# A state space layer between dense layers on one core: its stages in another order, and the norm factor applied when two of its quarters leave PSUM

## The chip, the cores and the metric

The kernel runs on one core of a Trainium2 chip. A core has a matrix engine (TensorE: PE in the profile, its weight loads PEld), a vector engine (VectorE: DVE), an engine for activations and copies (ScalarE: ACT), GpSimd (POOL) and a queue engine (SyncE: SP). Matrix products are written to PSUM, which VectorE and ScalarE read; everything else lies in SBUF or in HBM, and DMA queues of SP, ACT and POOL move data between these. The metric is the device time of one execution in microseconds (us), as the median of several runs; lower is better.

## The reference, cut to what matters

A sequence of 256 tokens of width 1024 goes through a stack of mixers and feed-forward layers. The third mixer is the state space layer:

```
def s5_layer(xn, w_in, ...):
    u = (xn @ w_in)                                   # 1024 channels = 64 groups of 16
    bu = einsum(bbar, u per group)                    # 64 complex states per group
    x[t] = a * x[t-1] + bu[t]                         # per group and state, over the tokens
    y = einsum(c_re, x_re) - einsum(c_im, x_im) + d_skip * u
    hg = gelu(y) @ w_glu
    a, g = split(hg, 2)
    return a * sigmoid(g)
```

`xn` is the RMS-normed input: `x` times a factor per token, times a gain per channel. The factor per token can be applied behind `@ w_in`, and the kernel does that.

## The kernel before, in words

**Dense products.** All matrix products with large weights run in three float32r passes. `mm3` (lines 514 to 518) multiplies a 128 x 128 block by a high and a low part of the activations, and the low part of the block by the high part of the activations, 256 tokens each. A *unit* is 8 blocks (512 KB). Units are loaded in the order of the list `s.plan` from SP's queue into five staging buffers `st`. A unit that isn't *raw* is then split into `wh` by ScalarE (line 374) and `wl` by VectorE (line 375), which frees its staging buffer; a raw unit is read by TensorE from the staging buffer and holds it until then.

**Who orders the work.** The program is written as one sequence of instructions. A list scheduler puts each engine's instructions in order: of those that are ready in its own plan of time it takes the one that stands first in the program, so a later one can move ahead while an earlier one waits. Each engine then runs its instructions strictly in that order. `keep_in_program_order` (not used in the layer before) forbids that an instruction is put ahead of the one that stands just before it on its engine. Matmuls into one PSUM bank stay in program order.

**The state space layer** (`s5`, lines 1205 to 1344) treats the 1024 channels as four quarters q of 256 channels (16 groups), and as two halves h of two quarters. `S5SEQ` (line 49) is the order of its stages, and `plan_s5` (line 1164) lists the weight units in the same order:

- **G q** (`g_stage`, line 1235): u = yh, yl times `w_in` for one quarter, 16 blocks. ScalarE copies PSUM to `uT` in another column order (line 1249), its queue stores that in HBM (`dU`, line 1250), and POOL's queue loads it back as `U8[q]` (line 1252), which turns the layout: tokens in steps of eight go to the partitions.
- **R** (`r_stage`, line 1227): the norm factor per token, `rrow` (256 values on every partition), and `r8`, the same in the layout of `U8`.
- **B q** (`b_stage`, line 1255): `U8[q]` times `r8` (VectorE, line 1258); 32 small products with raw units of `dB` into `Z` (line 1266); then a chain of eleven VectorE operations (lines 1273 to 1287): a turn by cosine and sine, two scans, a turn back, and the states written to `S[q]`. Its tiles `a`, `b`, `d` exist once, so the chains of two quarters can't overlap.
- **T h** (`y_mm(h, True)`, line 1299): what tokens within a group of eight do to each other, from `U8` of both quarters of the half, into `Y[h]`.
- **C h** (`y_mm(h, False)`, line 1303): the part from the states, `S` of both quarters, with raw units of `dC`, added to `Y[h]`.
- **F h** (`fin`, line 1306): gelu of `Y[h]` (ScalarE, line 1309), then for each half b of the tokens 4 products with the identity into the one buffer `pz` (line 1314), and from there the high and low parts `oh`, `ol` (`hilo`, lines 542 and 543). The second b needs `pz` back.
- **O** (`glu`, line 1323): the product with `w_glu`, 128 blocks (384 matmuls). The blocks stand in `glu_order` (line 138): 24 blocks that need only the first half of `oh`, for three output tiles; 24 that need the second half, for the same tiles; then the other five tiles. The three tiles hold the three PSUM buffers `mm` until their second 24 blocks are done. `ev_g` (line 1332) makes the result of a tile and adds it to `x`.

The next layer's feed-forward product follows; its matmuls need `x`.

Of the kernel before, what the change touches and what calls it, by code (L numbers as in the profile page):

```python
# [14 lines left out]
OP = mybir.AluOpType  # L15
# [30 lines left out]
PSTEP = (24, 36)  # L46
FSIDE = ((0.2, 0.8, 15), (1.6, 0.2, 16))
SIDE = (0, 1, 1.6, 0.6, 1.4, 0.2, 0.8, 1.0)
S5SEQ = [(x[0], int(x[1])) for x in "G0 G1 G2 R0 B0 G3 B1 T0 B2 B3 T1 C0 F0 C1 F1 O0 O1 O2".split()]
MAGIC = float(1.5 * 2 ** 23)  # L50
PI = float(np.pi)
INV2PI = float(1.0 / (2 * np.pi))
C1 = 6.28125
# [230 lines left out]
class Build:  # L284
# [879 lines left out]
    def plan_s5(s):  # L1164
        nc = s.nc
        s.dE = s.dp.tile([8, 64, 2, 64], F32, tag="dE", name="dE")
        s.dU = [s.dp.tile([8, 128, 64], F32, tag="dU%d" % q, name="dU") for q in range(4)]
        s.dB = s.dp.tile([8, 128, 8, 128], F32, tag="dB", name="dB")
        s.dC = s.dp.tile([8, 128, 8, 128], F32, tag="dC", name="dC")
        s.dK = s.dp.tile([64, 32, 2, 128], F32, tag="dK", name="dK")  # L1170
        def op(src, n):
            def f(st):
                s.pre_step(1e9)
                nc.sync.dma_start(st.rearrange("p (a n) -> p a n", a=n), src)
            return f

        for kind, q in S5SEQ:
            if kind == "G":
                for k in (2 * q, 2 * q + 1):
                    ap = s.I["s5in"]  # L1180
                    s.plan.append((ap[k], ap.shape[2], False))
            elif kind == "B":
                for k in (2 * q, 2 * q + 1):
                    s.plan.append((op(s.dB[k], 8), UW, True))
            elif kind == "C":
                v = s.dC[q * 4:q * 4 + 4].rearrange("k p g n -> p k (g n)")
                for m in range(4):
                    s.plan.append((op(v[:, :, m * 256:m * 256 + 256], 4), UW, True))
            elif kind == "O":
                for k in ((0, 3), (3, 6), (6, 16))[q:q + 1]:  # L1190
                    for u in range(*k):
                        s.plan.append((s.I["s5glu"][u], UW, False))

# [11 lines left out]
    def s5(s, nxt):  # L1205
        nc = s.nc
        mm = nc.tensor.matmul
        tt, stt = nc.vector.tensor_tensor, nc.vector.scalar_tensor_tensor
        with s.tc.tile_pool(name="s5", bufs=1) as fp, s.tc.tile_pool(name="s5w", bufs=1) as w5:
            f = lambda shape, tag, dt=F32: fp.tile(shape, dt, tag=tag, name=tag)  # L1210
            uT = [f([128, 1024], "uy%d" % h) for h in range(2)]
            uT = [uT[q // 2][:, (q % 2) * 512:(q % 2) * 512 + 512].rearrange("p (j k c) -> p j k c", j=8, k=2)
                  for q in range(4)]
# [21 lines left out]
            def g_stage(q):  # L1235
                P = s.ps().rearrange("p (k t) -> p k t", k=2)
                late = []
                for k in range(2):
                    for c in range(KC):
                        w = s.blk()  # L1240
                        if q or c < 6:
                            s.mm3(P[:, k], w, s.yh[:, c], s.yl[:, c], k == 0 and c == 0, c == KC - 1)
                        else:
                            late.append((k, c, w))
                    if q * 2 + k in NSTEP:
                        next(pre, None)
                for k, c, w in late:
                    s.mm3(P[:, k], w, s.yh[:, c], s.yl[:, c], False, c == KC - 1)
                nc.scalar.copy(uT[q].rearrange("p j k c -> p k j c"), P.rearrange("p k (c j) -> p k j c", j=8))
                nc.scalar.dma_start(s.dU[q].rearrange("j p n -> p j n"), uT[q].rearrange("p j k c -> p j (k c)"))  # L1250
                u = s.dU[q]
                nc.gpsimd.dma_start(U8[q].rearrange("p g k c -> p (g k c)"),
                                    bass.AP(tensor=u.tensor, offset=u.offset, ap=[[512, 16], [8192, 8], [1, 512]]))

            def b_stage(q):

                u = U8[q].rearrange("p g k c -> p (g k) c")
                tt(u, u, r8.unsqueeze(1).to_broadcast([128, 16, 32]), OP.mult)
                Z = (s.ps() if q % 2 else s.pz.tile([128, 512], F32, tag="pz", name="pz"))
                Z = Z.rearrange("p (r n) -> p r n", r=2)  # L1260
                for pr in range(8):
                    w = [s.blk(), s.blk()]
                    gg = pr * 2
                    for ri in range(2):
                        for half in range(2):
                            mm(Z[64 * half:64 * half + 64, ri, pr * 32:pr * 32 + 32],
                               w[half][:, ri * 64:ri * 64 + 64], U8[q][:, gg % 8 + half, gg // 8],
                               start=pr == 0 and ri == 0, stop=True, skip_group_check=True)
                sl = slice(q * 8, q * 8 + 8)
                Zv = Z.rearrange("p r (a c) -> p r a c", a=8)  # L1270
                cs, sn = [z[:, sl].unsqueeze(1).to_broadcast([128, 2, 8, 32]) for z in (s.s5cos, s.s5sin)]
                a, b, d = [w5.tile([128, 2, 8, 32], F32, tag=n, name=n) for n in "abd"]
                tt(b, Zv, cs, OP.mult)
                tt(d, Zv, sn, OP.mult)
                tt(a[:, 0], b[:, 0], d[:, 1], OP.add)
                tt(a[:, 1], b[:, 1], d[:, 0], OP.subtract)
                fl = lambda z: z.rearrange("p a c -> p (a c)")
                for r in range(2):
                    nc.vector.tensor_tensor_scan(fl(a[:, r]), fl(dec[:, sl]), fl(a[:, r]), 0.0, OP.mult, OP.add)
                Sv = S[q][:, :, 1:33].rearrange("p (a g) c -> p a g c", g=2)  # L1280
                R = [slice(0, 64), slice(64, 128)]
                tt(b, a, cs, OP.mult)
                tt(d, a, sn, OP.mult)
                for half, r in enumerate(R):
                    tt(Sv[0:64, :, half], b[r, 0], d[r, 1], OP.subtract)
                for half, r in enumerate(R):
                    tt(Sv[64:128, :, half], d[r, 0], b[r, 1], OP.add)

            def y_mm(h, direct):

                if direct:
                    Y[h] = s.zt().rearrange("p b (g n) -> p (b g) n", g=4)
                for g in range(8):
                    if not direct and g % 2 == 0:
                        w = s.unit()
                    for k in range(4):
                        q, e = 2 * h + k // 2, k % 2
                        if direct:
                            mm(Y[h][32 * k:32 * k + 32, g], U8[q][:, g, e], s.dT[h][:, k * 8 + g],
                               start=g % 4 == 0, stop=False, skip_group_check=True)  # L1300
                        else:
                            o = (k * 2 + g % 2) * 128
                            mm(Y[h][32 * k:32 * k + 32, g], S[q][:, e * 8 + g, 0:32], w[:, o:o + 128],
                               start=False, stop=True, skip_group_check=True)

            def fin(h):

                yg = f([128, 1024], "uy%d" % h).rearrange("p (j n) -> p j n", j=8)
                nc.scalar.activation(yg.rearrange("p j (g h) -> p g j h", g=8),
                                     Y[h].rearrange("p g (j h) -> p g j h", j=8), AF.Gelu_apprx_tanh)  # L1310
                for b in range(2):
                    P = s.pz.tile([128, 512], F32, tag="pz", name="pz")
                    for j in range(4):
                        mm(P[:, j * 128:j * 128 + 128], yg[:, b * 4 + j], s.c["ident"], start=j == 0, stop=True,
                           skip_group_check=True)
                    k, t = slice(4 * h, 4 * h + 4), slice(128 * b, 128 * b + 128)
                    v = lambda z: z[:, k, t].rearrange("p k (j c) -> p j k c", j=4)
                    s.hilo(v(oh), v(ol), P.rearrange("p (j k c) -> p j k c", j=4, k=4))
# [3 lines left out]

            def glu(k):

                for j, m, c in order[24 * k:24 * k + 24 if k < 2 else None]:
                    if j not in PG:
                        PG[j] = s.ps().rearrange("p (m t) -> p m t", m=2)
                    s.mm3(PG[j][:, m], s.blk(), oh[:, c], ol[:, c], m == 0 and c == 0, c == KC - 1)
                    if m and c == KC - 1:
                        ev_g(j, PG[j])  # L1330
# [614 lines left out]
```

## Time and profile before

| what | us |
|---|---|
| median of 3 runs (1617.16 to 1620.99) | 1618.54 |
| the profiled execution, device time | 1625.3 |
| the profiled execution, first to last instruction (the span all times below are counted from) | 1623.2 |
| first G stage to the last GLU tile, in that span | about 597 to 703 |
| TensorE busy, share of the span | 97% |

All rows come from the profiled execution. In a timeline a row is: start, duration, engine, line, operation, what it writes and reads, count; in brackets stands how long the engine was idle before it, and what released it. A record of a small matmul (lines 1266, 1299, 1303, 1314) is one of two passes, so 32 products give 64 records. The clock column of a table of windows (PEclk) is the granted clock of TensorE: 1.00 is 2.4 GHz, 0.50 is 1.2 GHz.

### The profile page before, as it was taken

Reading aid. Unit: us, or ns where it says so; the run is one execution under the profiler, and the core shown is the slowest. Engines: PE = TensorE matmul, PEld = TensorE weight load, DVE = VectorE, ACT = ScalarE, POOL = GpSimd, SP = SyncE. Lnnn points to the kernel's source line nnn. Section 1 sums busy time; section 2 is a strip of 40 time slices with the busy share of each in tenths; the row PEclk is TensorE's granted clock in tenths of the full one; section 3 lists DMA queues with packets and bytes.
Section 4 is the critical chain, followed back from the end, with each engine's and each line's share of the span. In section 5 each row is a group of like instructions: output and inputs, shape, how many; then the busy total and the mean of one; then the engine's idle time right before and its main releaser. Section 6 shows DMA issues by size and latency. Waiting matters only on the chain.

```text
span 1623.2 us, 33910 instructions
## 1 busy us (share of the span) xinstructions
PE 1573.0 (97%) x13644; PEld 1510.7 (93%) x13644; DVE 1303.4 (80%) x2380; ACT 948.1 (58%) x1481; POOL 64.1 (4%) x110
## 2 busy tenths in 40 slices
PE   7999999989999997999999999999999999999998
PEld 6999999979898996999999999999997899999998
DVE  8989998979889887788888567988886667766667
ACT  6777565645446661665556676656665546554444
POOL 0320100011110000000000000000000000000000
PEclk9999999999999998999999999999999999999999
DMA  7655666597986657746555434565553434656662
GB/s 262 202 181 176 230 212 223 201 279 228 244 245 227 219 186 221 258 165 215 195 195 184 167 118 157 190 200 195 173 171 125 151 119 132 202 193 195 194 196 79
DMA packets 95229, 312.54 MB, mean 193 GB/s; under 512 B 14928, under 2 KB 20560, under 8 KB 95072
## 3 DMA queue, kind: packets, MB, share of 16 engines
q1 hardware_dynamic: 82560, 282.21, 52.5%
q0 software_dynamic: 8352, 27.12, 5.9%
q8 instruction: 107, 1.75, 0.4%
q10 hardware_dynamic: 4160, 1.05, 0.3%
q14 instruction: 50, 0.41, 0.1%
HBM read 297.49 MB, written 12.85 MB: 191 GB/s over the span
## 4 chain that ended last, share of the span: by engine, by line
PE 72%; issue 10%; DVE 9%; DMA 6%; ACT 3%; POOL 0%; DVEq 0%; ACTq 0%; POOLq 0%; SPq 0%
PE mm L516 16%; PE mm L517 15%; PE mm L518 15%; PE z L516 5%; PE z L517 5%; PE z L518 5%; DVE wl L375 3%; DMA st<-ffn_dram 2%; DMA A<-s5bT_dram 2%; PE mm L530 1%; PE mm L531 1%; PE mm L529 1%; ACT wh L374 1%; PE z L818 1%; PE z L805 1%
## 5 line engine op out<-in xcount | busy, mean ns | idle before, releaser
L375 DVE TENSOR_TENSOR wl<-st,wh 128x1024 fp32r<-128x1024 f32 x508 | 617.1, 1218 | 156.9 <-ACT wh L374 156.1
L374 ACT CAST wh<-st 128x1024 fp32r<-128x1024 f32 x508 | 528.6, 1046 | 338.8 <-PE mm L517 206.8
L516 PE MATMUL mm<-yh,wh 128*128 128x256 f32 x2512 | 702.8, 280 | 1.6 <-ACT yh L568 0.9
L518 PE MATMUL mm<-yh,wl 128*128 128x256 f32 x2512 | 698.0, 278 | 4.4 <-DVE wl L375 4.4
L517 PE MATMUL mm<-yl,wh 128*128 128x256 f32 x2512 | 697.4, 278 | 1.0 <-DVE yl L569 0.6
L516 PEld LDWEIGHTS mm<-yh,wh 128*128 128x128 f32 x2512 | 472.6, 188 | 9.2 <-issue 6.0
L518 PEld LDWEIGHTS mm<-yh,wl 128*128 128x128 f32 x2512 | 473.2, 188 | 5.6 <-DVE wl L375 5.4
L517 PEld LDWEIGHTS mm<-yl,wh 128*128 128x128 f32 x2512 | 473.3, 188 | 2.5 <-DVE yl L569 1.0
L516 PE MATMUL z<-hh,wh 128*128 128x256 f32 x880 | 243.7, 277 | 0.0
L517 PE MATMUL z<-hl,wh 128*128 128x256 f32 x880 | 243.3, 276 | 0.4 <-DVE hl L543 0.4
L518 PE MATMUL z<-hh,wl 128*128 128x256 f32 x880 | 242.4, 276 | 1.3 <-DVE wl L375 1.3
L518 PEld LDWEIGHTS z<-hh,wl 128*128 128x128 f32 x880 | 164.9, 188 | 1.5 <-DVE wl L375 1.5
L516 PEld LDWEIGHTS z<-hh,wh 128*128 128x128 f32 x880 | 165.1, 188 | 1.1 <-issue 0.4
L517 PEld LDWEIGHTS z<-hl,wh 128*128 128x128 f32 x880 | 165.2, 188 | 0.7 <-DVE hl L543 0.6
L727 DVE SCALAR_TENSOR_TENSOR cv<-pr,conv,cv 128x255 f32<-128x255 f32 (+1 forms) x352 | 146.8, 477 | 1.3 <-ACT cv L725 0.9
L542 ACT CAST hh<-hm 128x256 fp32r<-128x256 f32 x110 | 44.5, 405 | 124.0 <-DVE hm L732 99.0
L725 ACT ACTIVATE cv<-pr,conv 128x256 f32<-128x256 f32 x176 | 95.8, 593 | 14.7 <-DVE pr L722 14.7
L516 PE MATMUL mm<-oh,wh 128*128 128x256 f32 x320 | 89.9, 282 | 0.0
L517 PE MATMUL mm<-ol,wh 128*128 128x256 f32 x320 | 88.3, 277 | 0.0
L518 PE MATMUL mm<-oh,wl 128*128 128x256 f32 x320 | 88.2, 277 | 0.0
L722 DVE TENSOR_TENSOR pr<-mm,rrow 128x512 f32<-128x512 f32 x88 | 60.1, 687 | 13.2 <-PE mm L518 12.9
L543 DVE TENSOR_TENSOR hl<-hm,hh 128x256 fp32r<-128x256 f32 x110 | 45.9, 420 | 24.3 <-ACT hh L542 24.3
(453 smaller groups left out, 1841.3 us busy)
## 6 DMA issues: line engine op xcount, KB each, us to landing
st<-ffn_dram SPq DMA_DIRECT2D x264, 512.0 KB, 4.2
st<-ffnx_dram SPq DMA_DIRECT2D x66, 512.0 KB, 3.7
st<-sbqk_dram SPq DMA_DIRECT2D x32, 512.0 KB, 4.3
st<-sbv_dram SPq DMA_DIRECT2D x16, 512.0 KB, 4.5
st<-sbo_dram SPq DMA_DIRECT2D x16, 512.0 KB, 3.5
st<-s5glu_dram SPq DMA_DIRECT2D x16, 512.0 KB, 5.4
st<-m_g_dram SPq DMA_DIRECT2D x16, 512.0 KB, 3.6
st<-ple_dram SPq DMA_DIRECT2D x10, 512.0 KB, 4.2
```

The costliest lines, as they stand in the source:

```text
L374: a = s.nc.scalar.copy(t[1][:, :n], t[0][:, :n])
L375: b = s.nc.vector.tensor_tensor(t[2][:, :n], t[0][:, :n], t[1][:, :n].bitcast(F32), OP.subtract)
L516: s.pinned(mm(P, w[0], xh, start=st, stop=False, skip_group_check=True))
L517: mm(P, w[0], xl, start=False, stop=False, skip_group_check=True)
L518: mm(P, w[1], xh, start=False, stop=sp, skip_group_check=True)
L529: s.pinned(mm(P[t][:, :width], a, w[0], start=c == 0, stop=False))
L530: mm(P[t][:, :width], a, w[1], start=False, stop=False)
L542: s.nc.scalar.copy(h, src)
L543: s.nc.vector.tensor_tensor(l, src, h.bitcast(F32), OP.subtract)
L722: nc.vector.tensor_tensor(pr, P, s.rrow.unsqueeze(1).to_broadcast([128, 2, T]), OP.mult)
L725: nc.scalar.activation(hc[:, m], pr[:, m], AF.Identity, bias=w(m, 3), scale=w(m, 2))
L727: nc.vector.scalar_tensor_tensor(hc[:, m, k:], pr[:, m, :T - k], w(m, 2 - k), hc[:, m, k:], OP.mult, OP.add)
```

## The change

The order of the stages changes: C0 goes ahead of B3, F0 ahead of T1, and the GLU's first 24 blocks (now in two pieces of 16 and 8) around C1. For quarters 2 and 3 the evacuation is done by VectorE, which multiplies by `rrow` on the way (two instructions of 256 columns), and the multiply of `U8` by `r8` falls away. The first matmul of C1, the first of each half of F1 and the first of O1 are kept behind the matmul that stands before them in the program.

```
-S5SEQ = "G0 G1 G2 R0 B0 G3 B1 T0 B2 B3 T1 C0 F0 C1 F1 O0 O1 O2"
+S5SEQ = "G0 G1 G2 R0 B0 G3 B1 T0 B2 C0 B3 F0 T1 O0 C1 O1 F1 O2 O3"
...
# plan_s5
-                for k in ((0, 3), (3, 6), (6, 16))[q:q + 1]:
+                for k in ((0, 2), (2, 3), (3, 6), (6, 16))[q:q + 1]:
...
# g_stage
-                nc.scalar.copy(uT[q].rearrange("p j k c -> p k j c"), P.rearrange("p k (c j) -> p k j c", j=8))
+                ov, pv = uT[q].rearrange("p j k c -> p k j c"), P.rearrange("p k (c j) -> p k j c", j=8)
+                if q < 2:
+                    nc.scalar.copy(ov, pv)
+                else:
+                    for k in range(2):
+                        tt(ov[:, k], pv[:, k], s.rrow.rearrange("p (c j) -> p j c", j=8), OP.mult)
...
# b_stage
-                tt(u, u, r8.unsqueeze(1).to_broadcast([128, 16, 32]), OP.mult)
+                if q < 2:
+                    tt(u, u, r8.unsqueeze(1).to_broadcast([128, 16, 32]), OP.mult)
...
# y_mm, the part from the states
+                            ins = mm(Y[h][32 * k:32 * k + 32, g], S[q][:, e * 8 + g, 0:32], w[:, o:o + 128], ...)
+                            if h and g == 0:
+                                s.tc.keep_in_program_order(ins)
...
# fin
+                        if h and j == 0:
+                            s.tc.keep_in_program_order(ins)
...
# glu
-                for j, m, c in order[24 * k:24 * k + 24 if k < 2 else None]:
+                s.pin = k == 1
+                for j, m, c in order[(0, 16, 24, 48)[k]:(16, 24, 48, None)[k]]:
```

## Rows read from the trace of the kernel before

**Rows 1.** The page's first part: busy time, share of the span, instructions.

```profile
PE 1573.0 (97%) x13644; PEld 1510.7 (93%) x13644; DVE 1303.4 (80%) x2380; ACT 948.1 (58%) x1481; POOL 64.1 (4%) x110
```

**Rows 2.** Table of windows: window, length, busy PE PEld DVE ACT POOL, PEclk, DMA, GB/s.

```profile
630.70:635.20 4.50, 0.00 (x0) 0.01 (x1) 0.78 (x2) 0.00 (x0) 0.00 (x0) 0.66 0.90 250
...
658.30:705.20 46.90, 46.86 (x414) 46.66 (x412) 38.19 (x52) 28.98 (x45) 0.00 (x0) 1.00 0.68 233
```

**Rows 3.** TensorE's timeline: C0's first records, B3, F0's two halves, F1's first.

```profile
629.55 1.05 PE L1303 MATMUL z<-st,S 128*32 128x128 f32 x16 [1.61 <-DMA st<-dC]
635.22 1.07 PE L1266 MATMUL mm<-U,st 128*64 128x32 f32 x16 [4.62 <-DVE U L1258]
...
643.24 1.16 PE L1314 MATMUL pz<-cst,uy 128*128 128x128 f32 x8 [1.12 <-ACT uy L1309]
646.75 2.08 PE L1314 MATMUL pz<-cst,uy 128*128 128x128 f32 x8 [2.35 <-DVE ol L543]
...
653.51 1.16 PE L1314 MATMUL pz<-cst,uy 128*128 128x128 f32 x8
```

**Rows 4.** Windows of lines 1266 (B0, B3) and 1303 (C0, C1): PE, PEld, clock.

```profile
613.90:616.10 2.20, 2.06 (x64) 1.95 (x64) 1.00 0.59 182
...
635.20:638.90 3.70, 3.63 (x64) 3.52 (x64) 0.50 0.20 56
...
640.30:642.20 1.90, 1.70 (x52) 1.53 (x52) 1.00 0.79 255
648.70:652.50 3.80, 3.63 (x60) 2.94 (x60) 0.50 0.42 134
```

**Rows 5.** The chain that ended last, behind G3's last matmul: start, us, what.

```profile
621.77 0.59 ACT uy L1249
...
622.38 4.31 DMA dU<-uy
...
627.22 7.18 DMA U<-dU
```

**Rows 6.** VectorE's timeline: multiplies (L1258), B1's chain, casts of F0, ev_g.

```profile
616.04 0.69 DVE L1258 TENSOR_TENSOR U<-U,r 128x512 f32<-128x512 f32 x1 [3.80 <-DMA U<-dU]
...
623.02 0.69 DVE L1258 TENSOR_TENSOR U<-U,r 128x512 f32<-128x512 f32 x1
623.76 0.69 DVE L1273 TENSOR_TENSOR b<-mm,s5cos 128x512 f32<-128x512 f32 x1
...
629.26 0.87 DVE L1287 TENSOR_TENSOR S<-d,b 64x256 f32<-64x256 f32 x2
634.42 0.69 DVE L1258 TENSOR_TENSOR U<-U,r 128x512 f32<-128x512 f32 x1 [4.29 <-DMA U<-dU]
...
646.01 0.68 DVE L543 TENSOR_TENSOR ol<-pz,oh 128x512 fp32r<-128x512 f32 x1
...
669.24 0.68 DVE L1338 SCALAR_TENSOR_TENSOR x<-hm,x 128x256 f32<-128x256 f32 x1
```

**Rows 7.** Groups by line and form in the layer: busy us, mean ns, idle before.

```profile
L542 ACT CAST oh<-pz 128x512 fp32r<-128x512 f32 x4 | 2.3, 581 | 5.1 <-PE pz L1314 5.1
...
L1282 DVE TENSOR_TENSOR b<-a,s5cos 128x512 f32<-128x512 f32 x4 | 2.8, 692 | 0.1
...
L1275 DVE TENSOR_TENSOR a<-b,d 128x256 f32<-128x256 f32 x4 | 1.7, 425 | 0.1
...
L1273 DVE TENSOR_TENSOR b<-pz,s5cos 128x512 f32<-128x512 f32 x2 | 1.4, 682 | 0.0
```

**Rows 8.** Reloads of U: landing; SP's one load behind C0's first; window at 632.

```profile
DMA to landing us min/median/max: 3.2/3.6/7.2
...
630.64 0.36 SPq L1174 DMA_DIRECT2D st<-dC  x1
...
632.00:634.00 2.00, 0.00 (x0) 0.00 (x0) 0.00 (x0) 0.00 (x0) 0.00 (x0) 0.54 1.08 303
```

**Rows 9.** TensorE's groups by form, 652.2 to 658.3: GLU blocks, one pass of three.

```profile
L518 PE MATMUL mm<-oh,wl 128*128 128x256 f32 x10 | 2.8, 278 | 0.0
```

More of the change, by code (lines that the diff above doesn't have):

```diff
@@ L48 @@
 SIDE = (0, 1, 1.6, 0.6, 1.4, 0.2, 0.8, 1.0)
-S5SEQ = [(x[0], int(x[1])) for x in "G0 G1 G2 R0 B0 G3 B1 T0 B2 B3 T1 C0 F0 C1 F1 O0 O1 O2".split()]
+S5SEQ = [(x[0], int(x[1])) for x in "G0 G1 G2 R0 B0 G3 B1 T0 B2 C0 B3 F0 T1 O0 C1 O1 F1 O2 O3".split()]
 MAGIC = float(1.5 * 2 ** 23)
@@ L1302, in y_mm @@
                             o = (k * 2 + g % 2) * 128
-                            mm(Y[h][32 * k:32 * k + 32, g], S[q][:, e * 8 + g, 0:32], w[:, o:o + 128],
-                               start=False, stop=True, skip_group_check=True)
+                            ins = mm(Y[h][32 * k:32 * k + 32, g], S[q][:, e * 8 + g, 0:32], w[:, o:o + 128],
+                                     start=False, stop=True, skip_group_check=True)
+                            if h and g == 0:
+                                s.tc.keep_in_program_order(ins)
             def fin(h):
@@ L1313, in fin @@
                     for j in range(4):
-                        mm(P[:, j * 128:j * 128 + 128], yg[:, b * 4 + j], s.c["ident"], start=j == 0, stop=True,
-                           skip_group_check=True)
+                        ins = mm(P[:, j * 128:j * 128 + 128], yg[:, b * 4 + j], s.c["ident"], start=j == 0, stop=True,
+                                 skip_group_check=True)
+                        if h and j == 0:
+                            s.tc.keep_in_program_order(ins)
                     k, t = slice(4 * h, 4 * h + 4), slice(128 * b, 128 * b + 128)
```

## The prediction, made before the changed kernel was run

> **What bounds the kernel now.** I read the page first: TensorE is busy for 97% of the span [rows 1], so a change can only win where TensorE waits or runs slowly. Next came a table by stretches of the state space layer [rows 2]. From 630.70 to 635.20 TensorE does nothing, and from 658.30 on it has no hole (46.86 of 46.90 us busy). So the change can win at most what the layer loses ahead of 658.3. TensorE's own timeline [rows 3] puts sizes on that. It waits 1.61 us for the first C weights, 4.62 us for the last quarter's U, 1.12 us for the gelu and 2.35 us for the first half's low part: 9.70 us. After the long waits it also runs at the lower of its two clocks (granted 0.50, 1.2 GHz): B3 takes 3.63 us, where B0 took 2.06 us for the same 64 records at 1.00; C1 takes 3.63 us, where 52 records of C0 took 1.70, so 64 about 2.1 [rows 4]; one half of F0 takes 2.08, the halves of F0 and F1 at full clock 1.16 [rows 3]. That is 1.57 + 1.5 + 0.9 = 4.0 us, so about 13.7 us in all, or 0.85% of the time.
>
> The chain that ended last says what these waits hang on [rows 5]: G3's evacuation (0.59 us), its store (4.31 us) and its reload (7.18 us). VectorE shows the second half of the story [rows 6]: the multiply of the last quarter's U stands in its queue ahead of B2's chain, so that chain, whose input B2's matmuls leave before TensorE goes to C0 at 629.55, begins only behind the multiply at 634.42.
>
> **The change, step by step.** One chain of a B stage on VectorE is 623.76 to 630.13 (its last pair begins at 629.26 and takes 0.87): 6.37 us [rows 6].
>
> *Evacuation of quarters 2 and 3.* ScalarE's copy becomes two VectorE multiplies of 256 columns, PSUM and a strided rrow in. No such row exists. Below stands 0.42 us for 256 plain columns [rows 7], above 0.68 us for 256 columns strided by eight, in and out [rows 6]; I take 0.55, midway, since input is strided and output is not: 1.1 us, bounds 0.84 and 1.36. Reading PSUM adds nothing in the trace: 682 ns from PSUM, 692 ns from SBUF for 512 columns [rows 7]. [...] Quarter 2's pair runs at 614, in VectorE's wait for U before 616.04 [rows 6]. If it is queued behind that multiply instead, its U comes some 3 us later, when B2 has that long in hand and TensorE next waits for S[1] anyway: nothing. ScalarE's saved copies are worth nothing: the layer gives it nothing else to do before the gelu. Quarter 3's pair is ready at 621.8, but VectorE is in B0's chain until 623.0 (the multiply behind it begins at 623.02 [rows 6]): it ends at 624.1, where the copy ended at 622.36 [rows 5]. Store and reload follow 1.75 us later.
>
> *The multiplies that go.* Quarter 3's costs the path 0.82 us (landing 634.40 to B3 at 635.22 [rows 3, 5]). B3 can so start at 635.22 + 1.75 - 0.82 = 636.15. I leave the reload at 7.18 us. Quarter 2's multiply at 623.02 makes room for quarter 3's pair, so B1's chain starts at 624.1 and ends at 630.5. B2's chain then follows at once and ends at 636.9 instead of 641.4.
>
> *C0 ahead of B3.* Its weights move ahead of B3's two units on SP's queue, so they lie there before S[1] does; B3's second unit, issued once C0's first is read at 631, is wanted in the middle of B3, at 638: as long as the longest landing here took, 7.2 us [rows 8]. C0 starts with S[1] at 630.5 and takes 2.1 us: 632.6. A quarter of it (16 records at 629.55 [rows 3]) was early before, so that part isn't gained. TensorE waits from 632.6 to 636.15: 3.55 us. B3 is then slow again, 3.63 us, since the wait before it is near the old 4.62: 639.8.
>
> *F0, T1, O0.* F0's first half 1.16 us (640.95); T1 2.1 us (643.05) covers the casts of that half; second half 1.16 us (644.2). Its casts, 0.58 on ScalarE [rows 7] and 0.68 on VectorE [rows 6] with 0.1 of hand-over, find VectorE in B3's chain and wait half an operation, 0.35 us (at 646.01 such a subtraction went in between two of its operations); behind the whole chain it would be 1.6 us more. O0 starts at 645.9: 48 matmuls at 0.113 us (46.86 over 414 [rows 2]) make 5.4: 651.3.
>
> *C1, O1, F1.* S[3] is ready at 639.8 + 6.37 + 0.7 = 646.9 and has 4 us of slack, which also holds the weight splits on VectorE; C1 2.1 us (653.4) at the full clock. O1, 24 matmuls, 2.7 us (656.1), covers the gelu's 1.12. F1's first half ends at 657.3. Here the new order pays: before, O0 filled the wait between F1's halves and the one behind them (653.51 on [rows 3]). Now O0 and O1 are used up, and O2 needs F1. Each wait is 1.36 us at best, by the casts above; before it was 2.35 between the halves of F0, with other work of VectorE in front [rows 3]. I take 1.9 twice: second half at 659.2 to 660.35, O2 at 662.25.
>
> *Clock.* Waits of 1.7 and 3.8 us in all are left. Of the two places before with a low clock, one had 1.61 and 4.62 us of waiting, the other 1.12 and 2.35 around a burst of 1.16 [rows 3]; the second resembles F1 now. Price: nothing to 2.4 us (1.5 + 0.9 above); I take 1.0. O2 stands at 663.25 by this count.
>
> *The sum.* By 658.33 the kernel before has done 10 blocks of the GLU [rows 9]; to do the 24 of O0 and O1 it needs 14 x 3 x 0.113 = 4.75 us more, so it stands at 663.1. The change is 0.15 us behind: 15 us of waiting and slow clock become 15. From there on TensorE has no hole, so this carries to the end. The profiled execution took 1625.3 us around a span of 1623.2; the median of the runs is 1618.54, 6.8 lower, and I add the difference to that: 1618.7.
>
> **Rivals.** *Faster: the planner puts F0 into the wait for U.* The gelu is ready 1.12 us behind C0, at 633.7. If F0's first half is issued ahead of B3, it ends at 634.9 inside the wait, its second half follows B3, and T1 covers the last casts: 1.16 + 1.7 = 2.9 us less. If quarter 3's pair also slips in before the last operations of B0's chain, its U is 1.2 us earlier. Together -4.1: 1614.6. For it: the subtraction at 646.01 and C0's 16 records show that the planner fills waits. Against: the program has B3 ahead of F0, and in the plan of before B3 came after just 16 records of C0, so the plan thinks U is there early.
>
> *Slower: the reload of the last quarter's U is crowded out.* Once C0 is read, SP may issue three more units (both of O0, the first of C1) at 631 to 632, while U is on its way; before, one load was issued there, at 630.64 [rows 8]. Reloads took 3.2 to 7.2 us, and the longest is this one, with the DMA share at 1.08 and 303 GB/s. If the three go ahead, 3 x 512 KB at 303 GB/s are 5.2 us; TensorE waits for all of it. Slower by over 0.2% from 3.1 us on; 1623.9 in full. Against: the loads issued ahead of U, which it already shares the engines with, are as many as before. [...]
>
> *It does less than it says.* If VectorE gets quarter 3's pair only behind more of other work, or O0 waits for the end of B3's chain (+1.6), the time is 1619 to 1621: within the no-change case.
>
> **Chances.** A difference of 0.2% is 3.2 us, about what measuring this kernel can tell from none. No change, 1618.7: 0.48, own range 1616 to 1621.5. Faster rival 0.30, for it and for F1 waits at 1.36 without a low clock (-2.1). Slower rival 0.22. Range 1614.2 to 1622.8: it takes in the faster rival's full size and most of the slower one's.
>
> **What the next profile shows.** Right: a wait before B3 of 3 to 4 us, B2's chain begun near 630.5, no operation on VectorE between U's landing and B3, a hole of 1.4 to 2.4 us before and after F1's second half. Wrong: F0 ahead of B3; U landing after 638 or before 635; O matmuls between F1's halves; or a difference that starts outside the layer.

## The result and the profile after

The changed kernel takes 1631.15 us (median of 4 runs, 1630.68 to 1633.73), the kernel before on the same chip 1619.57 (1617.16 to 1620.99). The ratio is 1.0076 [1.0059, 1.0094]: slower by some 12 us, and outside the range of the prediction. One of the ten executions of the kernel e7 below took 3158.47 us in a slow state, and its median and ratio leave that one out.

The new line numbers: the VectorE evacuation is L1254, the reload of U L1257, B's products L1272, B's chain L1279 to L1293, T L1305, C L1309, gelu L1317, F's products L1322. In the kernels of the experiments these lines lie up to six apart.

**Where the time went.** One row for the whole layer, from one column sum (L584) on TensorE to the next, first of the kernel before, then of the kernel after; then three stretches of the latter, two at the low clock and the one in which O0 runs (window, length, busy PE PEld DVE ACT POOL, PEclk, DMA, GB/s):

```profile
603.85:705.15 101.30, 90.79 (x1112) 87.27 (x1111) 75.46 (x129) 39.81 (x58) 3.05 (x5) 0.93 0.72 235
```

```profile
599.54:711.68 112.14, 95.49 (x1111) 90.82 (x1110) 76.27 (x131) 38.44 (x56) 3.06 (x5) 0.89 0.66 213
...
626.89:637.13 10.24, 6.45 (x106) 5.35 (x108) 6.92 (x14) 1.02 (x1) 0.52 (x1) 0.50 0.51 175
...
643.95:654.19 10.24, 7.63 (x32) 7.04 (x33) 6.42 (x13) 1.53 (x2) 0.95 (x1) 0.50 0.50 160
...
648.37:657.19 8.82, 8.55 (x52) 8.13 (x56) 3.19 (x6) 1.94 (x2) 0.00 (x0) 0.67 0.21 70
```

The layer is 10.84 us longer with the same matmuls, and two columns say how. Length less busy PE is TensorE's idle time: 10.51 us before, 16.65 after, +6.14. Busy PE itself rose by 4.70: the same work at a lower clock (0.89 on the mean against 0.93). Behind the layer the two traces take 918.05 and 917.52 us; ahead of it 603.85 and 599.54, the same instructions, with a low clock (0.50) for 6.8 us at 356 in the one and not in the other. In the trace of the kernel after, matmuls of 256 columns start 0.213 us apart at 0.50 (649.82 to 654.08) and 0.113 us apart at 1.00 (655.44 to 656.91), which is 1.20 and 2.27 columns per ns. No view shows a clock in GHz: the 1.2 and 2.4 GHz ahead of this section can be read as the first of these rates and its double. The page's busy line hardly shows the loss; PE has 2.5 us more than in [rows 1]:

```profile
PE 1575.5 (97%) x13644; PEld 1512.2 (93%) x13644; DVE 1303.9 (80%) x2382; ACT 947.3 (58%) x1479; POOL 64.3 (4%) x110
```

**TensorE's timeline after**, to be laid beside [rows 3] (times 4.31 us earlier for the same work ahead of the layer):

```profile
627.33 0.66 PE L1309 MATMUL z<-st,S 128*32 128x128 f32 x8 [2.79 <-DVE S L1293]
631.33 0.43 PE L1305 MATMUL z<-dT,U 128*32 128x128 f32 x2 [3.35 <-DMA U<-dU]
...
635.74 1.74 PE L1272 MATMUL mm<-U,st 128*64 128x32 f32 x32
...
638.40 1.13 PE L1272 MATMUL mm<-U,st 128*64 128x32 f32 x32
639.46 1.16 PE L1322 MATMUL pz<-cst,uy 128*128 128x128 f32 x8
640.54 0.64 PE L1305 MATMUL z<-dT,U 128*32 128x128 f32 x14
...
645.62 2.08 PE L1322 MATMUL pz<-cst,uy 128*128 128x128 f32 x8 [4.44 <-DVE ol L543]
...
648.37 0.80 PE L516 MATMUL mm<-oh,wh 128*128 128x256 f32 x2 [0.68 <-ACT oh L542]
...
661.85 1.05 PE L1322 MATMUL pz<-cst,uy 128*128 128x128 f32 x8
665.93 1.16 PE L1322 MATMUL pz<-cst,uy 128*128 128x128 f32 x8 [3.04 <-DVE ol L543]
667.76 0.53 PE L516 MATMUL mm<-oh,wh 128*128 128x256 f32 x1 [0.68 <-ACT oh L542]
```

Three things stand out. C0 (L1309) stops after 12 of its 64 records, for 3.35 us, at a T1 product (L1305), which the planner put inside C0 and which reads the last quarter's U: so most of C0 waits for U too, and B3 follows it in two halves, with T1 products between. F0's second half waits 4.44 us for the subtraction `ol`; 50 of T1's 64 records had run before F0's first half, and only the 14 that were left (0.64 us) stand in that wait. And F1 stands bare, with waits of 3.04 and 0.68 us.

**VectorE's timeline after** shows why `ol` is late (to be laid beside [rows 6]):

```profile
620.19 1.17 DVE L1254 TENSOR_TENSOR uy<-mm,rrow 128x256 f32<-128x256 f32 x2
...
639.57 0.69 DVE L1279 TENSOR_TENSOR b<-mm,s5cos 128x512 f32<-128x512 f32 x1 [5.49 <-PE mm L1272]
...
640.78 1.22 DVE L375 TENSOR_TENSOR wl<-st,wh 128x1024 fp32r<-128x1024 f32 x1
...
642.25 1.22 DVE L375 TENSOR_TENSOR wl<-st,wh 128x1024 fp32r<-128x1024 f32 x1
...
644.90 0.66 DVE L543 TENSOR_TENSOR ol<-pz,oh 128x512 fp32r<-128x512 f32 x1
...
648.69 0.69 DVE L543 TENSOR_TENSOR ol<-pz,oh 128x512 fp32r<-128x512 f32 x1
...
662.72 2.56 DVE L375 TENSOR_TENSOR wl<-st,wh 128x1024 fp32r<-128x1024 f32 x2 [5.41 <-ACT wh L374]
665.19 0.68 DVE L543 TENSOR_TENSOR ol<-pz,oh 128x512 fp32r<-128x512 f32 x1
```

F0's first half ended at 640.6, and VectorE had been idle for 5.49 us until 639.57. But its queue holds, ahead of `ol`, the first half of B3's chain and two weight splits (L375) of the GLU units that O0 needs early. At F1 two splits again stand ahead of `ol`.

### The profile page after: what moved, and what is told of

Same layout as the page of the kernel before. It is cut to its first block, busy times and chain, and to the rows that moved or that the text cites. A ratio compares the mean times of both kernels' runs of the same rounds, so it can differ in the third digit from the quotient of the medians.

```text
span 1629.2 us, 33904 instructions
## 1 busy us (share of the span) xinstructions
PE 1575.5 (97%) x13644; PEld 1512.2 (93%) x13644; DVE 1303.9 (80%) x2382; ACT 947.3 (58%) x1479; POOL 64.3 (4%) x110
## 3 DMA queue, kind: packets, MB, share of 16 engines
q10 hardware_dynamic: 4160, 1.05, 0.3%
## 4 chain that ended last, share of the span: by engine, by line
PE 55%; DVE 2%; ACT 1%; DMA 1%; issue 0%; ACTq 0%; POOLq 0%
PE mm L516 12%; PE mm L517 12%; PE mm L518 12%; PE z L516 4%; PE z L517 4%; PE z L518 4%; PE mm L531 1%; PE mm L529 1%; PE mm L530 1%; DVE wl L375 1%; PE z L1712 0%; PE z L818 0%; ACT wh L374 0%; PE z L1699 0%; PE z L805 0%; PE pz L1466 0%
## 5 line engine op out<-in xcount | busy, mean ns | idle before, releaser
L375 DVE TENSOR_TENSOR wl<-st,wh 128x1024 fp32r<-128x1024 f32 x508 | 617.2, 1218 | 166.0 <-ACT wh L374 165.3
L516 PEld LDWEIGHTS mm<-oh,wh 128*128 128x128 f32 x320 | 61.7, 194 | 3.7 <-ACT oh L542 1.8
```

Source lines behind the costliest of these rows:

```text
L375: b = s.nc.vector.tensor_tensor(t[2][:, :n], t[0][:, :n], t[1][:, :n].bitcast(F32), OP.subtract)
L516: s.pinned(mm(P, w[0], xh, start=st, stop=False, skip_group_check=True))
```

## The experiments

Three theories went in. **A**: the planner's orders cost it (the T1 product inside C0 on TensorE; B3's chain and the splits ahead of F0's casts on VectorE). **B**: the evacuation on VectorE brings the last quarter's U late. **C**: the new tail costs it (O0, C1, O1, F1: nothing is left to fill F1's waits, early splits stand in the way, and O0 falls into a low clock). The early splits belong to A, as a matter of the planner's order, and to C, as that of units wanted early. All results in one table. The layer is measured from L584 to L584 in each profiled execution; idle is its length less busy PE. The ratio is to runs of the kernel before on the same chip (medians 1619.5 to 1620.7). Each layer is that of one execution, and no kernel's layer was profiled twice. What isn't the layer (the profiled device time less the layer) took from 1514.71 us (e4) to 1525.34 (e5) for the same instructions, so a difference of one or two microseconds between two layers may be chance.

| kernel | median us | ratio | layer | PE busy | idle |
|---|---|---|---|---|---|
| before | 1619.57 | | 101.30 | 90.79 | 10.51 |
| after | 1631.15 | 1.0076 [1.0059, 1.0094] | 112.14 | 95.49 | 16.65 |
| e1 before + evacuation | 1621.85 | 1.0010 [0.9997, 1.0023] | 101.24 | 90.26 | 10.98 |
| e2 after − evacuation | 1630.33 | 1.0068 [1.0051, 1.0085] | 109.65 | 93.03 | 16.62 |
| e3 after, T1 behind C0 | 1629.61 | 1.0057 [1.0037, 1.0077] | 109.73 | 94.21 | 15.52 |
| e4 after, old tail | 1622.25 | 1.0010 [0.9998, 1.0022] | 103.64 | 90.88 | 12.76 |
| e5 before, new tail | 1634.13 | 1.0080 [1.0053, 1.0106] | 110.46 | 95.44 | 15.02 |
| e6 after, O1 in F1 | 1634.22 | 1.0081 [1.0050, 1.0112] | 110.18 | 93.04 | 17.14 |
| e7 = e3 + e6 + F0 first | 1623.28 | 1.0020 [1.0003, 1.0037] | 103.41 | 91.07 | 12.34 |
| e8 = e4 + T1 behind C0 | 1619.56 | 0.9993 [0.9978, 1.0008] | 100.29 | 91.42 | 8.87 |
| e9 = e3 + F0 first | 1624.01 | 1.0025 [1.0008, 1.0041] | 105.38 | 95.44 | 9.94 |
| e10 = e7, O0 of 8 blocks | 1621.37 | 1.0001 [0.9988, 1.0015] | 101.79 | 92.19 | 9.60 |
| e11 = e8 + F0 first | 1622.43 | 1.0007 [0.9994, 1.0021] | 103.12 | 91.47 | 11.65 |
| e12 before, new tail, O1 in F1 | 1629.40 | 1.0062 [1.0041, 1.0082] | 107.08 | 93.34 | 13.74 |

### The evacuation: with nothing else, and undone (e1, e2)

e1 takes the kernel before and puts in the two edits below; e2 takes the changed kernel and puts them back.

```
-                nc.scalar.copy(uT[q]..., P...)
+                if q < 2: nc.scalar.copy(ov, pv)
+                else: tt(ov[:, k], pv[:, k], s.rrow..., OP.mult)   # k = 0, 1
...
-                tt(u, u, r8..., OP.mult)
+                if q < 2: tt(u, u, r8..., OP.mult)
```

> The kernel before with one part of the change alone: quarters 2 and 3 leave PSUM through VectorE, times rrow, and their multiply behind the reload is gone; order of stages and GLU as before. Theory A (the loss is made by the order in which the planner laid out TensorE's and VectorE's queues): the last quarter's store starts some 3 us later, but B2's chain no longer stands behind its multiply, so the end of the layer is 0 to 2 us earlier than before: 1617 to 1620. Theory B (the loss is the late store and reload of the last quarter): 3 us or more slower than before, 1623 to 1626, with B3 at least 3 us later in the layer. Theory C (the loss is at the tail: nothing left to fill the waits behind F1, and the low clock): no difference from before.

> The changed kernel with the other part alone: the new order of stages, the GLU in four pieces and the pinned matmuls, but all quarters evacuated by ScalarE and multiplied behind the reload, as before. Theory A: nearly the whole loss, 1627 to 1632; T1's first products that need the last quarter's U stand inside C0 or before B3 again, and F0's casts stand behind weight splits on VectorE. Theory B: at most half of the loss, 1620 to 1625. Theory C: nearly the whole loss, 1627 to 1632, with waits behind both halves of F1.

e1 can't be told from the kernel before, by the runs or by the layer (101.24 against 101.30); e2 keeps nearly the whole loss. Theory B falls as the cause of the loss. That the evacuation does nothing is not shown. In e1, whose layer begins at 597.01, the store of the last quarter began 22.28 us into the layer, where it began 18.53 us into it before [rows 5]. The reload then took 3.61 us, where it took 7.18 before; that and the multiply saved make up for the delay:

```profile
619.29 5.04 DMA dU<-uy
624.85 3.61 DMA U<-dU
```

In the ten kernels with the new evacuation TensorE could read the last quarter's U 31.5 to 35.2 us into the layer, in the four without it (before, e2, e5, e12) 30.0 to 31.4. So it does bring U later. And e2's layer is 2.49 us shorter than that of the changed kernel, nearly all of it busy PE, while the intervals of their runs overlap. In e2 U came before C0 was through, the T1 products that need it stood at C0's end and met no wait, and B3 ended 35.6 us into the layer against 40.0 in the changed kernel. F0's second half then waited even longer:

```profile
645.96 2.08 PE L1316 MATMUL pz<-cst,uy 128*128 128x128 f32 x8 [6.09 <-DVE ol L543]
```

So the loss doesn't need a late B3.

### T1 kept out of C0 (e3)

```
+                            if h and g == 0 and k == 0:
+                                s.tc.keep_in_program_order(ins)   # first T1 product
```

> The changed kernel with T1 kept behind F0 on TensorE (its first product is pinned to the one before it in the program), so that no product that waits for the last quarter's U stands inside C0. Theory A: C0 ends some 5 us earlier than in the changed kernel, B3's second unit is issued 4 to 5 us earlier and B3 ends 3 to 4 us earlier; what F0's casts lose behind the splits on VectorE stays, so the time is 1626 to 1629. The slower rival of the prediction, seen here: with C0 done early, SP issues the loads of the GLU while U is on its way, and the reload takes 6 us or more instead of 4.2. Theories B and C: no change from the changed kernel, 1630 to 1633.

The layer is 2.41 us shorter than in the changed kernel, and by the runs the loss is nearly all still there. TensorE now reads C0 before U comes. But U comes late, and F0's second half waits longer than in the changed kernel: all of T1 now runs behind it (from 646.76 on), so nothing stands in that wait. The timeline:

```profile
634.14 3.63 PE L1272 MATMUL mm<-U,st 128*64 128x32 f32 x64 [1.58 <-DMA U<-dU]
...
644.76 2.07 PE L1324 MATMUL pz<-cst,uy 128*128 128x128 f32 x8 [4.98 <-DVE ol L543]
```

In the chain that ended last the store and reload of the last quarter read:

```profile
621.36 4.21 DMA dU<-uy
626.09 8.01 DMA U<-dU
```

So the part of theory A that concerns TensorE shows in the layer and is small; the runs, whose intervals overlap, don't show it. U's reload took 8.01 us here, with four loads of SP issued while it ran (at 628.35, 628.79, 629.25 and 632.62).

### The old tail behind the new head, and the new tail behind the old head (e4, e5)

```
e4: S5SEQ = "G0 G1 G2 R0 B0 G3 B1 T0 B2 C0 B3 F0 T1 C1 F1 O0 O1 O2"
e5: S5SEQ = "G0 G1 G2 R0 B0 G3 B1 T0 B2 B3 T1 C0 F0 O0 C1 O1 F1 O2 O3"
```

e4 has the new evacuation and no pins, and its GLU pieces are as before; e5 has the old evacuation, the three pins and the new pieces.

> The changed kernel with the old tail: behind T1 come C1, F1 and then the whole GLU in three pieces, and nothing is pinned; evacuation and the order up to T1 are as in the changed kernel. Theory C: most of the loss goes, 1620 to 1624. Theory A: T1 inside C0 still costs its 4 to 5 us, but without splits of GLU weights in front of F0's casts and with GLU products between F1's halves 4 to 6 us come back: 1625 to 1627. Theory B: no change from the changed kernel but for the waits behind F1 (some 4 us): 1627.

> The kernel before with nothing but the new tail: its own evacuation and multiplies, B2, B3, T1, C0, F0 in the old order, then O0, C1, O1, F1 with the three pins and the GLU's first 24 blocks in pieces of 16 and 8. Theory C (the tail loses: nothing left to fill F1's waits, and the early GLU units' splits stand ahead of F0's casts on VectorE): 1627 to 1630, with a wait of 2 to 6 us before F0's second half, about 3 and 0.7 us around F1's second half. Theory A (the loss needs the T1 product inside C0, so it is the head that loses): within 2 us of the kernel before, 1619 to 1622.

This pair decides it. The new head alone lengthens the layer by 2.34 us, the new tail alone by 9.16; together 11.50, where the change as a whole measured 10.84. Theory C holds, by the runs too: 1.0010 and 1.0080. The pair moves the order, the pieces and the pins of the tail together and doesn't part them. In e4's timeline F0's second half waits 0.63 us, and C1 then waits for the last quarter's states, since no GLU block stands ahead of it:

```profile
637.20 1.16 PE L1320 MATMUL pz<-cst,uy 128*128 128x128 f32 x8 [0.63 <-DVE ol L543]
642.26 3.49 PE L1309 MATMUL z<-st,S 128*32 128x128 f32 x60 [3.90 <-DVE S L1293]
```

e5 came out beyond the 1627 to 1630 expected. In it no T1 product stands in C0 ahead of B3 and the wait for U is 1.17 us, and TensorE still waits for F's work at every turn; the layer's row, then TensorE's timeline:

```profile
603.51:713.97 110.46, 95.44 (x1111) 91.28 (x1110) 75.52 (x129) 39.79 (x58) 3.05 (x5) 0.89 0.66 217
```

```profile
643.23 1.16 PE L1316 MATMUL pz<-cst,uy 128*128 128x128 f32 x8 [2.67 <-ACT uy L1311]
647.23 2.08 PE L1316 MATMUL pz<-cst,uy 128*128 128x128 f32 x8 [2.84 <-DVE ol L543]
...
666.58 1.16 PE L1316 MATMUL pz<-cst,uy 128*128 128x128 f32 x8 [2.82 <-DVE ol L543]
668.41 1.01 PE L516 MATMUL mm<-oh,wh 128*128 128x256 f32 x3 [0.68 <-ACT oh L542]
```

Even the gelu is later than in [rows 3] (2.67 us against 1.12), and ScalarE's timeline shows that an early weight split stands ahead of it, and behind that the load of the gelu's table (1.28 us), which before ran at 622.84 in ScalarE's idle time:

```profile
639.80 1.05 ACT L374 CAST wh<-st 128x1024 fp32r<-128x1024 f32 x1 [16.48 <-DMA st<-s5glu_dram]
640.86 1.28 ACT L1311 ACT_TABLE_LOAD   x1
642.16 1.02 ACT L1311 ACTIVATE uy<-z 128x1024 f32<-128x1024 f32 x1
```

The busy PE of the layer is 4.65 us above that of the kernel before, as in the changed kernel, while e4, with the old tail, has 90.88. Over all kernels it is 90.26 to 91.47 with the old tail and 91.07 (e7) to 95.49 with the new one: the added low clock comes with the tail, though not in every form of it.

### O1 back into F1's waits (e6, e12)

```
-... O0 C1 O1 F1 O2 O3      (F1 and O1 pinned)
+... O0 C1 F1 O1 O2 O3      (neither pinned)
```

e6 does this to the changed kernel, e12 to e5.

> The changed kernel with one thing undone: F1 stands ahead of O1 in the program and neither is pinned, so that O1's 24 matmuls can go into the waits around F1's halves. Theory C, part one: F1's waits of 3.04 and 0.68 us and some 1.7 us of slow clock behind them shrink by 3.5 to 5.5 us: 1625.5 to 1627.5. If F1's waits are only where a delay shows that lies elsewhere (the casts stuck behind weight splits, whoever fills the wait): within 1.5 us of the changed kernel, 1629.5 to 1632.

> The kernel before with nothing but the new tail, and F1 ahead of O1 and unpinned, so that O1's 24 matmuls go between F1's halves. A third pair for the price of F1's waits: without O1 there the layer took 110.46 us and the runs 1634.13. If F1's empty waits cost what the two profiled pairs gave (1.96 and 1.97 us): the layer takes 108 to 109 us, 1629 to 1633. If another part of the tail takes it over (O0 behind F0's casts at the low clock), the layer stays at 110 to 111 and the runs at 1632 to 1636.

In e6 the wait between F1's halves is shorter, and F0's is as long as ever:

```profile
641.95 2.08 PE L1322 MATMUL pz<-cst,uy 128*128 128x128 f32 x8 [5.09 <-DVE ol L543]
...
659.58 1.16 PE L1322 MATMUL pz<-cst,uy 128*128 128x128 f32 x8 [1.26 <-DVE ol L543]
```

The layer gains 1.96 us, but the runs gain nothing (1.0081 against 1.0076): outside both figures I had given. The profiled execution of e6, with 1625.79 us, is the fastest of its four, and the others lie at 1633.37 to 1635.67, so its layer need not be theirs. e12 gains 3.38 us of the layer and has 1.0062 against 1.0080, inside what was expected of its runs and better than that in its layer. A third pair, e7 against e9, gains 1.97 us of the layer and 1.0020 against 1.0025, though U came 2.85 us later in e7's layer than in e9's. So O1 there is worth 2.0 to 3.4 us in the profiled layers and from 1 us lost to 3 us won by the ratios, whose intervals are wider than that. It seems a part, and not the largest; the runs don't settle it.

### F0's casts ahead of the splits and of B3's chain (e9, e7)

```
-... C0 B3 F0 T1 O0 ...
+... C0 F0 B3 T1 O0 ...     (first T1 product pinned, as in e3)
```

e9 keeps the changed kernel's tail and pins, so it stands beside e3. e7 has e6's tail besides.

> The changed kernel with T1's first product pinned behind F0 and F0 ahead of B3 in the program; O0, C1, O1, F1 and their pins are as in the changed kernel. Beside the run that only pins T1 this moves F0's casts ahead of B3's chain and of the weight splits on VectorE. If the casts behind that work are the largest single part (the layer takes 109.73 us with T1 pinned and 103.41 with O1 among F1's halves as well): the layer takes 104.5 to 106.5 us and 1623 to 1626, with F1's waits of about 3 and 0.7 us still there and hardly any slow clock in O0. If O0 runs slowly for another reason than the wait before it: 1628 to 1631.

> The same as the run with O1 between F1's halves, and further F0 ahead of B3 in the program, T1's first product pinned behind F0: F0's first half can run while TensorE waits for the last quarter's U, and its casts stand ahead of B3's chain and of the splits on VectorE. Theory C, all parts: 5 us from F1, 1.5 us from T1, 4 us from F0's casts and the clock: 1619 to 1621.5. If the slower rival of the prediction takes over (the reload of U grows to 8 us once SP issues more loads beside it): B3 starts 3 us later and 1622 to 1625 are left.

e9 lies where it was expected if these casts are the largest single part: 1624.01 and 105.38 us, 4.35 us of the layer less than e3, the largest step by a single move. On VectorE the first `ol` now follows one operation of the chain, the second comes before the chain's third:

```profile
637.24 0.69 DVE L1279 TENSOR_TENSOR b<-mm,s5cos 128x512 f32<-128x512 f32 x1 [4.92 <-PE mm L1272]
637.85 0.68 DVE L543 TENSOR_TENSOR ol<-pz,oh 128x512 fp32r<-128x512 f32 x1
638.44 1.22 DVE L375 TENSOR_TENSOR wl<-st,wh 128x1024 fp32r<-128x1024 f32 x1
...
640.18 1.21 DVE L375 TENSOR_TENSOR wl<-st,wh 128x1024 fp32r<-128x1024 f32 x1
641.79 0.69 DVE L543 TENSOR_TENSOR ol<-pz,oh 128x512 fp32r<-128x512 f32 x1 [0.40 <-ACT oh L542]
```

On TensorE F0's second half comes with no wait, O0 follows at the full clock (its matmuls start 0.11 to 0.12 us apart from 642.76 on), and F1's wait is untouched:

```profile
634.13 2.08 PE L1324 MATMUL pz<-cst,uy 128*128 128x128 f32 x8
...
637.13 2.77 PE L1305 MATMUL z<-dT,U 128*32 128x128 f32 x42
639.83 1.30 PE L1324 MATMUL pz<-cst,uy 128*128 128x128 f32 x8
642.54 0.39 PE L517 MATMUL mm<-ol,wh 128*128 128x256 f32 x1 [0.19 <-DVE ol L543]
...
656.69 1.61 PE L1324 MATMUL pz<-cst,uy 128*128 128x128 f32 x8 [2.92 <-DVE ol L543]
```

The move does two things, and e9 doesn't part them. From the end of F0's first half to the end of its `ol` it takes 2.3 us here, against 4.9 in the changed kernel and in e3: that is the order in VectorE's queue. The 2.3 us are filled on TensorE by the rest of B3 and 42 records of T1, which in e3 stood elsewhere.

e7's layer takes 103.41 us, but its runs, at 1623.28, lie above the 1619 to 1621.5 expected and inside the 1622 to 1625 that I had given for a late U. B3 begins 4.21 us after TensorE's last work, behind a reload of 7.24 us. That reload is no longer than the 7.18 us before [rows 5]; the store ahead of it began 2.3 us later in the layer and took 6.53 us, where it took 4.31:

```profile
636.73 2.98 PE L1272 MATMUL mm<-U,st 128*64 128x32 f32 x50 [4.21 <-DMA U<-dU]
```

### Looking for a version that beats both (e8, e10, e11)

```
e8:  e4 with the first T1 product pinned
e10: e7 with O0 of 8 blocks (one unit), 16 left for O1
e11: e8 with F0 ahead of B3
```

> The new head with the old tail, as in the run before of that kind, and T1's first product pinned so that no T1 product stands inside C0. If the T1 product is worth what pinning it gave under the new tail, 1.5 us: 1620.5 to 1621. If C0's early end only lets SP issue loads beside the reload of U (about 8 us then): no gain, 1622 to 1624.

> The run with F0 first and O1 among F1's halves, with O0 cut from 16 blocks to 8 (one unit), so that 16 are left for F1's waits, and only one unit's splits are early. Candidate for a version that beats both. If the weight loads beside it set how long the reload of U takes: U lands in 4 to 5 us, the layer takes 98 to 100 us, 1616 to 1618.5. If the reload stays at 8 us: the layer takes 101 to 102.5 us, 1619.5 to 1621.5.

> The run with the new head, the old tail and T1 pinned, and F0 ahead of B3 besides. Its layer took 100.29 us, with 1.40 us before F0's second half. That wait goes, since F0's halves are parted by T1 products: layer 98.5 to 100, 1617 to 1619.5, if TensorE doesn't then wait that much longer for the last quarter's states (0.46 us there); if it does, 100 to 101 and 1619 to 1620.5.

e8 came out below its 1620.5 to 1621, 2.69 us under e4 (on another chip; the intervals of the two ratios overlap), and its layer is 3.35 us shorter: in the layers, with the old tail, the T1 product inside C0 was worth more than the new head had lost. Its layer is the shortest of all, 1.01 us below that of the kernel before, but 0.9993 [0.9978, 1.0008] is no difference that can be told. Its row, then F0's second half and the bulk of C1:

```profile
595.86:696.15 100.29, 91.42 (x1112) 87.54 (x1111) 76.39 (x131) 38.27 (x56) 3.05 (x5) 0.93 0.73 238
```

```profile
635.30 2.07 PE L1322 MATMUL pz<-cst,uy 128*128 128x128 f32 x8 [1.40 <-DVE ol L543]
640.36 2.08 PE L1311 MATMUL z<-st,S 128*32 128x128 f32 x60 [0.46 <-DVE S L1293]
```

e10 took 1621.37 us, in its less hopeful case, though U's reload took 5.1 us and not 8; e11, with 1622.43, lies above both of its cases. In both a wait only moved: with F0's wait gone, C1 waits for the last quarter's states, 1.32 us in e10 and 3.02 in e11. No version here beats the kernel before by more than can be measured.

## Why the prediction was wrong

The stages after, moved by 4.31 us onto the times of the prediction:

| | predicted | after | off by |
|---|---|---|---|
| B3 ends | 639.8 | 643.84 | +4.0 |
| O0 starts | 645.9 | 652.68 | +6.8 |
| O0 ends | 651.3 | 661.50 | +10.2 |
| O1 ends | 656.1 | 666.32 | +10.2 |
| O2 starts | 662.25 | 672.07 | +9.8 |

The terms, in the prediction's order:

- *Evacuation.* Right in price: the two pairs took 1.14 and 1.17 us (taken 1.1, bounds 0.84 and 1.36). (One of the two takes 0.61 to 0.63 us, some 0.2 above a plain 0.42 us row; how much of that is the strided operand and how much the PSUM source no run here parts. The 512-column multiplies by the same cosine took 686 and 692 ns from PSUM, L1279, and 688 from SBUF, L1288, in the kernel after.) Its place in VectorE's queue was mis-sized: B0's chain, ahead of it, ended 1.5 us later in the layer than before, and quarter 3's pair ended at 625.67 on the prediction's times, not 624.1. That U could still be read at 635.64, close to the 636.15 forecast, is luck: the reload took 4.2 us, not the 7.18 taken.
- *The multiplies that go* and *C0 ahead of B3*: **the first step that failed**, 4.0 us. I had C0 run whole at S[1] and B3 at full length behind U. The planner set a T1 product that needs U inside C0. So C0 waited for U, B3's second unit was issued only at 632.44, once C0's first unit had been read, and B3 came in halves. Part of the 4.0 us is T1's work done early (46 of its 64 records ran between U's landing and B3's end), and C0, T1 and B3's first half ran at 0.50. The rows had shown that this planner interleaves such products (16 records of C0 stood ahead of B3 [rows 3]); I used that to price a gain and didn't ask what one early product blocks in an engine that runs its queue in order (TensorE stood at it for 3.35 us, with 52 records of C0 behind it). By the layers of e3 and e8 the T1 product is worth 2.4 us under the new tail and 3.35 under the old one. It isn't the whole loss: in e2 B3 ended 35.6 us into the layer, where the forecast had 36.0, and the kernel still took 1630.33 us.
- *F0, T1, O0*: **the second**, 2.8 us more. I gave F0's casts "half an operation, 0.35 us" of B3's chain in front. What stood there was half the chain and two splits of 1.22 us, and TensorE waited 4.44 us. T1, which the prediction had covering these casts with 2.1 us, was used up by then but for 0.64 us. The early units O0 and O1 bring their splits with them: I had put these, on VectorE, into the 4 us of slack that the states of quarter 3 would have, and not ahead of F0's casts, and had none on ScalarE. e9 takes the wait away by moving F0 ahead (VectorE's order and T1's place together), and e5 shows that the loss needs neither the new evacuation nor the new order of C0.
- *Clock*: **the third**, mis-sized. I took 1.0 us, bound 2.4. O0's 48 matmuls took 8.82 us instead of 5.4, and the first 3.4 us of O2 ran at 0.50 too. The layer's busy PE rose by 4.70 us, where the prediction had it fall by 1.4: of the 4.0 us of slow clock before, it kept B3's 1.57 and the 1.0. That is some 6.1 us of the 10.7 by which the layer missed, and it stands inside the steps above: the first has a low clock from 626.89 to 637.13, the second from 643.95 on. The low clock after the wait before F0's second half now falls on O0, where before it fell on C1 and half of F0 [rows 4].
- *C1, O1, F1*: right for C1, 1.95 us at the full clock (2.1), and O1, 3.0 (2.7). F1's two waits, 3.04 and 0.68, come to 3.72 against 1.9 twice, but that is luck: the first is longer, since two splits stood ahead of `ol`, and the second shorter, since O2 starts on `oh` alone (its first matmul at 667.76, where `ol` ended at 668.74).

As for the rivals: the faster one (F0 inside the wait for U) didn't happen in the changed kernel. When e9 came near it, F0's first half was done in the middle of B3, and the kernel was still slower than before. The slower one had the reload of U grow beyond 7.18 us by up to 5.2. In the changed kernel it took about 4.2 us (issued by POOL at 627.10, read at 631.33), so it wasn't the cause there, and the longest seen is e3's 8.01. The nearest to what happened is what the prediction had called no change, "O0 waits for the end of B3's chain (+1.6)", but it was F0's second half that waited, behind half of that chain and two splits.

What stays open: how much of the tail's 9.16 us each part has by itself. e3, e9 and e7 take 2.41, 4.35 and 1.97 us off the changed kernel's layer and lead to 103.41; the last 2.1 us to the kernel before weren't taken apart. Nor is it shown how much of e9's step is VectorE's order and how much T1's new place, or what the late store of the new evacuation costs where U is waited for.

## What to carry to other kernels

Where a scheduler writes each engine's queue, a stage moved ahead in the program brings all that its weights need, on every engine (here splits of 1.22 us on VectorE and, in e5, of 1.05 on ScalarE): ask of each wait that you forecast what will stand in that engine's queue just ahead of the instruction waited for. One early product that needs the late input turns a whole stage that doesn't need it into one that does (here C0, for 3.35 us). And filler work that is moved leaves its old wait open: here the GLU's 24 early blocks were moved from F1's waits to the wait for the states, and a wait of 3.04 us came back at F1 (what that one costs by itself the runs don't settle).

## What the runs showed that I had not expected

- Less idle time doesn't mean less time. e9 has less idle than the kernel before (9.94 against 10.51 us) and 4.65 us more busy PE, with a mean granted clock of 0.90 in the layer against 0.93. Both columns of a layer's row have to be read:

```profile
598.14:703.52 105.38, 95.44 (x1111) 90.61 (x1110) 76.41 (x131) 38.35 (x56) 3.06 (x5) 0.90 0.69 227
```

- The reload of the same 256 KB took 3.61 us (e1), 4.29 (e8), 7.24 (e7) and 8.01 (e3), and the number of loads issued beside it doesn't settle this: e8 had four units issued while it ran (624.41 to 626.65), e3 four as well. What makes 8.01 of the one and 4.29 of the other no run here shows.
